# FoX attention on one core: masks of five of eight diagonal blocks moved into copies of the gates, and the low halves of K kept in fixed slots

## The chip, the core and the metric

The kernel runs on one core of a Trainium2 chip. Times are microseconds of device time of one execution; three runs of the kernel before gave a median of 2348.22 (2346.97 to 2348.58). A profile is one further execution, recorded by the hardware: it names each instruction's engine, line, start and duration. The engines are PE (TensorE: matrix products, with its weight loads PEld), DVE (VectorE), ACT (ScalarE), POOL (GpSimd) and SP, which here only issues transfers (DMAs). Each engine works through its own list of instructions in order, and waits at semaphores for the others.

## What is computed

A trunk of two layers over 1024 frames of width 1024, in float32: layer 0 mixes by FoX attention, layer 1 by gated linear attention (GLA), each followed by a SwiGLU layer, all with RMS norm and adaLN modulation from a vector c. The change is in the FoX attention, 16 heads of 64:

```python
log_f = jax.nn.log_sigmoid(f_logit.astype(jnp.float32) + b_f.astype(jnp.float32))
cum = jnp.cumsum(log_f, axis=1).transpose(0, 2, 1)
scale = FOX_HEAD_DIM ** -0.5
for blk in range(S // Q_BLOCK):
    qs, qe = blk * Q_BLOCK, (blk + 1) * Q_BLOCK
    logits = jnp.einsum('bqhd,bkhd->bhqk', q[:, qs:qe], k[:, :qe]).astype(jnp.float32) * scale
    logits = logits + cum[:, :, qs:qe, None] - cum[:, :, None, :qe]
    mask = (qs + jnp.arange(Q_BLOCK))[:, None] >= jnp.arange(qe)[None, :]
    logits = jnp.where(mask[None, None], logits, -jnp.inf)
    p = jax.nn.softmax(logits, axis=-1).astype(v.dtype)
    outs.append(jnp.einsum('bhqk,bkhd->bqhd', p, v[:, :qe]))
```

Query block qb (0 to 7) of 128 rows sees the key blocks 0 to qb; only the last of them, the diagonal block of 128 x 128, needs the mask.

## The kernel before

**Heads and units.** Heads come in pairs p = 0 to 7, with a = 0, 1 for the two heads of a pair, so head h = 2p + a. `attention(p)` goes through the units of a head in the order g = 0, 3, 1, 2 (`ORDER`); a unit holds the query blocks 2g and 2g + 1. So a head goes through blocks 0, 1, then 6, 7, then 2, 3, then 4, 5, and block 5 is the last. The outputs of a unit are held back (`pending`) until the scores of the next unit stand in the program.

**A block's scores.** `scores` cuts the keys of a block into pieces of at most 512 columns (block 4 into 384 and 256; blocks 5 to 7 into 512 and the rest). Each piece is made by two products, Q with the high half of K (L1292, tiles KA or KB for the two heads of a pair) and with the low half (L1293, KLA or KLB). The tiles of K are 128 rows high, of which the other head's 64 rows are zero. A piece that ends with the diagonal block gets a third product on PE, identb times maskb (L1295), which adds 1e30 above the diagonal. DVE then adds the gates, a row of cum spread over 128 partitions, takes the running minimum and writes the piece to lp (L1298); ACT takes exp (L1302), DVE the reciprocal of the sum (L1303), POOL scales the block (L1304). PE transposes the scaled block (L1324, lp to t_b), ACT and DVE split it into a high and a low half (L174, L175, to pt), and PE multiplies with V (L1336, L1338, to o_b). Of o_b's two halves ACT copies one (L1352, to ot) and DVE adds the other and writes oT (L1353).

**What runs beside it.** `weave` lays the program of `attention(p)` and the projections of q, k and v for the next pair (qk_b, vps_b; L316 to L318) into one another by their estimated costs, and a scheduler then sets the final order on each engine. The projections split their weights into halves (L246, on POOL and DVE), `q_evac` and `k_evac` bring q and k out of PSUM (L867 to L883), and each call of `k_evac` writes zeros into the empty half of KLA and KLB first (L877, L878, POOL). Between them stands the modulation of the later parts, which multiplies loaded pieces of in_ada_w (L477, L479 on POOL, L516 on DVE, tiles ada and acc).

**Gates.** `load_cum` (L1119) lets SP load the row of one head, 1024 numbers spread over 128 partitions, 512 KB as written, into one of two buffers. It is called for heads 0 and 1 at the end of the gates, and for the two heads of the next pair after the program of a pair.

**Constants.** maskb holds 1e30 above the diagonal in bf16; tri is the 0/1 triangle that the GLA layer uses much later.

## Time and profile before

| | |
|---|---|
| median of three runs | 2348.22 us (2346.97 to 2348.58) |
| the profiled execution | 2348.03 us, of which 2346.3 is the span from its first to its last instruction |
| mean granted clock of PE | 0.995 |
| attention stage | about 98 to 600 us: the first mask product starts at 98.1, the last at 589.5 |
| mask products, L1295 | 128 loads of identb (96 ns each) and 128 products (230 ns each) |
| scaling of blocks, L1304 | 128 on POOL, 98.2 us |

In rows of the profile, an operation is written with its line, engine, what it writes, an arrow and what it reads, shapes and a count; tile names lose their numbers (lp_s, s_b, t_b: _s for SBUF, _b for PSUM). In timelines the first two columns are the start and the duration in us. What stands in brackets behind a row is the idle time of that engine before it and the instruction that ended it. The durations of products overlap, since PE starts the next one before the last has come out: two starts, not one duration, tell what a product costs.

### The profile page before, as it was taken

What the parts mean: (1) busy time and instruction counts of PE and PEld (TensorE: products, weight loads), DVE (VectorE), ACT (ScalarE), POOL (GpSimd) and SP (SyncE); (2) the same over time, 40 slices, a digit from 0 to 9 for tenths busy, and PEclk for the clock granted to TensorE, in tenths of its full rate; (3) what the DMA queues carried; (4) which work ended last, traced back from release to release, by engine and by line L of the source; (5) the groups of instructions that cost most, each with busy time, mean ns of one, the idle gap of its engine ahead of it and who ended that gap; (6) DMA issues with size and microseconds to landing.
All of it is one profiled execution on the core that took longest, in us unless ns stands there. A gap on an engine that the chain in (4) does not pass through costs nothing.

```text
span 2346.3 us, 35561 instructions
## 1 busy us (share of the span) xinstructions
PE 2326.5 (99%) x12168; PEld 1983.7 (85%) x12168; DVE 1779.5 (76%) x2947; ACT 1123.0 (48%) x2166; POOL 1142.8 (49%) x1005
## 2 busy tenths in 40 slices
PE   8999999999999999999999999999999999999999
PEld 7988888888888888888888899898888888888888
DVE  6577787877687888887788666568787777876787
ACT  6565665665544333345325654345444333345236
POOL 1334455533345656665563522335456666664651
PEclk8999999999999999999999999999999999999999
DMA  8423333432325545448774443554435544458774
GB/s 262 146 79 116 108 113 94 128 127 103 117 95 188 184 162 167 161 172 314 253 272 155 134 129 100 148 174 167 150 106 160 177 150 156 140 189 299 238 267 137
DMA packets 349615, 383.38 MB, mean 163 GB/s; under 512 B 25373, under 2 KB 286649, under 8 KB 349433
## 3 DMA queue, kind: packets, MB, share of 16 engines
q1 hardware_dynamic: 349432, 381.11, 49.3%
q8 instruction: 96, 1.57, 0.3%
q14 instruction: 87, 0.70, 0.1%
HBM read 279.76 MB, written 101.25 MB: 162 GB/s over the span
## 4 chain that ended last, share of the span: by engine, by line
PE 90%; DVE 3%; DMA 3%; issue 1%; SPq 1%; ACT 1%; POOL 1%; DVEq 0%; POOLq 0%; ACTq 0%
PE p_b L316 16%; PE p_b L318 16%; PE p_b L317 16%; PE o_b L1338 2%; PE t_b L1324 2%; PE qk_b L316 2%; PE qk_b L317 2%; PE qk_b L318 2%; PE vps_b L318 1%; PE vps_b L316 1%; PE vps_b L317 1%; PE gr_b L316 1%; PE s_b L1292 1%; PE s_b L1293 1%; PE gr_b L317 1%
## 5 line engine op out<-in xcount | busy, mean ns | idle before, releaser
L174 ACT CAST o_s<-xv_s 128x512 fp32r<-128x512 f32 (+1 forms) x392 | 236.5, 610 | 344.4 <-PE p_b L318 256.9
L175 DVE TENSOR_TENSOR o_s<-xv_s,o_s 128x512 fp32r<-128x512 f32 (+1 forms) x392 | 335.2, 860 | 42.6 <-ACT o_s L174 40.5
L318 PE MATMUL p_b<-B,o_s 128*128 128x512 f32 x608 | 236.0, 389 | 0.0
L317 PE MATMUL p_b<-B,o_s 128*128 128x512 f32 x608 | 235.9, 389 | 0.0
L316 PE MATMUL p_b<-B,o_s 128*128 128x512 f32 x608 | 235.4, 390 | 0.0
L1304 POOL TENSOR_SCALAR lp_s<-lp_s,st 128x128 f32<-128x128 f32 (+7 forms) x128 | 98.2, 771 | 246.1 <-DVE st L1303 231.2
L951 POOL TENSOR_TENSOR ex_s<-xv_s,xv_s 128x512 f32<-128x512 f32 (+1 forms) x64 | 95.6, 1494 | 238.3 <-DMA xv_s<-in_ffn_w_in_dram 118.4
L316 PE MATMUL p_b<-T,o_s 128*128 128x512 f32 x480 | 186.8, 389 | 0.0
L317 PE MATMUL p_b<-T,o_s 128*128 128x512 f32 x480 | 186.7, 389 | 0.0
L318 PE MATMUL p_b<-T,o_s 128*128 128x512 f32 x480 | 181.2, 389 | 0.0
L318 PEld LDWEIGHTS p_b<-B,o_s 128*128 128x128 f32 x608 | 114.1, 188 | 23.9
L316 PEld LDWEIGHTS p_b<-B,o_s 128*128 128x128 f32 x608 | 114.1, 188 | 23.7 <-DVE x L1670 0.2
L317 PEld LDWEIGHTS p_b<-B,o_s 128*128 128x128 f32 x608 | 114.2, 188 | 23.5
L1302 ACT ACTIVATE lp_s<-lp_s,st 128x128 f32<-128x128 f32 (+7 forms) x128 | 99.4, 777 | 57.2 <-DVE st L1298 55.8
L953 POOL TENSOR_TENSOR xv_s<-ex_s,xv_s 128x512 f32<-128x512 f32 (+1 forms) x64 | 94.5, 1477 | 58.9 <-DVE o_s L175 55.9
L1670 DVE TENSOR_TENSOR ex_s<-ex_s,p_b 128x512 f32<-128x512 f32 x140 | 94.2, 681 | 36.7 <-PE p_b L318 36.6
L174 ACT CAST pt_s<-t_b 128x512 fp32r<-128x512 f32 (+1 forms) x160 | 79.7, 547 | 73.7 <-PE t_b L1324 73.1
L963 POOL TENSOR_TENSOR xv_s<-xv_s,xv_s 128x512 f32<-128x512 f32 x48 | 65.5, 1365 | 92.7 <-issue 52.3
L246 POOL TENSOR_TENSOR w_l_s<-w__s,w_h_s 128x256 fp32r<-128x256 f32 x90 | 69.4, 800 | 84.3 <-ACT w_h_s L242 66.3
L175 DVE TENSOR_TENSOR pt_s<-t_b,pt_s 128x512 fp32r<-128x512 f32 (+1 forms) x160 | 96.3, 630 | 15.9 <-ACT pt_s L174 15.4
L318 PEld LDWEIGHTS p_b<-T,o_s 128*128 128x128 f32 x480 | 90.1, 188 | 18.7
L317 PEld LDWEIGHTS p_b<-T,o_s 128*128 128x128 f32 x480 | 90.1, 188 | 18.7
(1527 smaller groups left out, 7413.9 us busy)
## 6 DMA issues: line engine op xcount, KB each, us to landing
xv_s<-in_ffn_w_in_dram SPq DMA_DIRECT2D x176, 256.0 KB, 3.2
hid_B<-x SPq DMA_DIRECT2D x66, 512.0 KB, 2.8
ad_s<-in_ada_w_dram SPq DMA_DIRECT2D x384, 64.0 KB, 2.4
hid_T<-x SPq DMA_DIRECT2D x44, 512.0 KB, 2.9
xv_s<-in_ffn_w_out_dram SPq DMA_DIRECT2D x88, 256.0 KB, 3.8
ada_s<-in_ada_w_dram SPq DMA_DIRECT2D x96, 128.0 KB, 2.7
T2o<-hid_T SPq DMA_DIRECT2D x22, 512.0 KB, 6.6
T1o<-hid_T SPq DMA_DIRECT2D x22, 512.0 KB, 6.3
```

The source lines that it names most:

```text
L174: nc.scalar.copy(hi, src)
L175: nc.vector.tensor_sub(lo, src, hi.bitcast(F32))
L246: (nc.gpsimd if i < 3 else nc.vector).tensor_sub(lo[:, cs], rw[:, cs], hi[:, cs].bitcast(F32))
L316: nc.tensor.matmul(ps, ah, bh, start=start, stop=False, skip_group_check=chain)
L317: nc.tensor.matmul(ps, ah, bl, start=False, stop=False, skip_group_check=chain)
L318: nc.tensor.matmul(ps, al, bh, start=False, stop=stop, skip_group_check=chain)
L951: nc.gpsimd.tensor_add(s1, a21, a22)
L953: nc.gpsimd.tensor_sub(a11, s1, a11)
L963: nc.gpsimd.tensor_sub(r[A12], r[A12], r[A11])
L1302: nc.scalar.activation(lp, lp, AF.Exp, bias=mcur, scale=-1.0, accum_out=st[:, qi, 2:3])
L1304: nc.gpsimd.tensor_scalar(lp, lp, st[:, qi, 3:4], 1.0, op0=ALU.mult, op1=ALU.mult)
L1670: nc.vector.tensor_add(d, d if src is None else dest(G, src), ps)
```

## The change

The masks of query blocks 0, 1, 4, 5 and 7 are no longer added by a product. For those blocks the mask is added on POOL to a copy of the gates, so that DVE's one operation with the gates adds it along. `near` holds the gates of block 0, and of blocks 0 and 1, for query blocks 0 and 1; `far` holds those of key blocks 3, 4 and of 4, 5 for the last pieces of query blocks 4 and 5. Both exist once and are loaded anew for each head by two transfers each, as soon as the head before has used them. For block 7 the mask goes into the last 128 columns of the head's own row of cum. Blocks 2, 3 and 6 keep their product. The rows of cum are now loaded one head at a time, after the last unit of the head that used the buffer. One addition on POOL masks near (128x2x128), one far, and one the end of cum (128x128), for each head.

The low halves of K get fixed slots: KLA serves all pairs, KLB and a new KLC take turns, and their zeros are written once (for pairs 0 and 1). The result of ACT's copy L1352 is written straight into oT, and DVE adds onto it in place. near and far are reused in the GLA layer: tri is made there in near, the states Sf lie in far, and junk in near.

In numbers of instructions: PE loses 80 loads and 80 products; POOL loses 26 memsets and gains 48 additions; SP gains 64 transfers; DVE loses one copy; ACT's number stays.

```diff
@@ -168,7 +168,8 @@
     for q in range(4):
         nc.vector.memset(four[32 * q:32 * q + 32, q:q + 1], 1.0)
     maskb = cst.tile([P, P], BF16, name="maskb")
-    tri = cst.tile([P, P], I32, name="tri")
+    near_t = cst.tile([P, 3 * P], F32, name="near")
+    far_t = cst.tile([P, HALF], F32, name="far")
 
     def split(hi, lo, src):
         nc.scalar.copy(hi, src)
...
@@ -846,20 +841,25 @@
 
     SC = -(64 ** -0.5)
 
-    qk_at = {}
+    qk_at, kl, kl_sl = {}, {}, []
 
     def qk_tiles(p):
 
 
-        at = {nm: qk_free.popleft() for nm in ("QA", "QB", "KA")}
+        at = {nm: qk_free.popleft() for nm in ("QA", "QB")}
         if p:
             before = qk_at.pop(p - 1)
-            at.update(zip(("KB", "KLA", "KLB"), (before[nm] for nm in ("QA", "KA", "KLA"))))
-            qk_free.extend(before[nm] for nm in ("QB", "KB", "KLB"))
+            at.update(KA=before["QA"], KB=before["KA"])
+            qk_free.extend(before[nm] for nm in ("QB", "KB"))
         else:
-            at.update({nm: qk_free.popleft() for nm in ("KB", "KLA", "KLB")})
+            at.update({nm: qk_free.popleft() for nm in ("KA", "KB")})
+        new = {0: ("KLA", "KLB"), 1: ("KLC",)}.get(p, ())
+        for nm in new:
+            kl_sl.append(qk_free.popleft())
+            kl[nm] = big.tile([P, S], FR, tag=kl_sl[-1], name=nm)
         qk_at[p] = at
-        return {nm: big.tile([P, S], FR, tag=sl, name=f"{nm}{p}") for nm, sl in at.items()}
+        t = {nm: big.tile([P, S], FR, tag=sl, name=f"{nm}{p}") for nm, sl in at.items()}
+        return t | {"KLA": kl["KLA"], "KLB": kl["KLC" if p % 2 else "KLB"], "zero": [(kl[nm], nm != "KLA") for nm in new]}
 
     def q_evac(ps, t, hf):
         cs = hsl(hf)
@@ -874,8 +874,8 @@
     def k_evac(ps, t, hf):
         cs = hsl(hf)
         KA, KB, KLA, KLB = t["KA"], t["KB"], t["KLA"], t["KLB"]
-        nc.gpsimd.memset(KLA[64:128, cs].bitcast(F32), 0.0)
-        nc.gpsimd.memset(KLB[0:64, cs].bitcast(F32), 0.0)
+        for z, b in t["zero"]:
+            nc.gpsimd.memset((z[0:64, cs] if b else z[64:128, cs]).bitcast(F32), 0.0)
         nc.scalar.copy(KA[0:64, cs], ps[0:64, :])
         nc.scalar.copy(KB[64:128, cs], ps[64:128, :])
         nc.scalar.copy(KA[64:128, cs], ps[0:64, :])
@@ -1105,6 +1105,8 @@
         nc.sync.dma_start(cum_d, cum)
         load_cum(0)
         load_cum(1)
+        load_near(0)
+        load_far(0)
 
     def v_split(g, tp, ps):
         v = vring([P, 2, 4, 2, 64], FR, f"v{g}{tp}")
@@ -1115,8 +1117,34 @@
     cums = {}
 
     def load_cum(h):
-        cums[h] = cumr([P, S], F32, f"cum{h}")
-        nc.sync.dma_start(cums[h], cum_d[h].partition_broadcast(P))
+        if h < 16:
+            cums[h] = cumr([P, S], F32, f"cum{h}")
+            nc.sync.dma_start(cums[h], cum_d[h].partition_broadcast(P))
+
+    def load_near(h):
+        if h < 16:
+            for o, n in ((0, 1), (P, 2)):
+                nc.sync.dma_start(near_t[:, o:o + n * P], cum_d[h, 0:n * P].partition_broadcast(P))
+
+    def load_far(h):
+        if h < 16:
+            for o, b in ((0, 3), (2 * P, 4)):
+                nc.sync.dma_start(far_t[:, o:o + 2 * P], cum_d[h, b * P:(b + 2) * P].partition_broadcast(P))
+
+    def mask_near(h):
+        if h < 16:
+            mask_pair(near_t, 0)
+
+    def mask_far():
+        mask_pair(far_t, 1)
+
+    def mask_pair(t, b):
+        t = t.rearrange("p (b k) -> p b k", k=P)[:, b:b + 3:2]
+        nc.gpsimd.tensor_add(t, t, maskb.unsqueeze(1).to_broadcast([P, 2, P]))
+
+    def mask_last(h):
+        t = cums[h][:, 7 * P:]
+        nc.gpsimd.tensor_add(t, t, maskb)
 
 
 
@@ -1275,6 +1303,7 @@
         t = qkt[p]
         Qs, K1, KL = (t["QA"], t["KA"], t["KLA"]) if a == 0 else (t["QB"], t["KB"], t["KLB"])
         cm = cums[2 * p + a]
+        own = {0: near_t[:, 0:P], 1: near_t[:, P:], 4: far_t[:, 0:2 * P], 5: far_t[:, 2 * P:]}
         if g < 2:
             both = lpr([P, (4 * g + 3) * P], F32, f"lp{p}{a}{g}")
             lps = [both[:, 0:(2 * g + 1) * P], both[:, (2 * g + 1) * P:]]
@@ -1290,12 +1319,14 @@
                 early = u == (0, 0, 0)
                 diag = k1 == Wd
                 nc.tensor.matmul(ps, Qs[:, qs], K1[:, k0:k1], start=True, stop=False)
-                nc.tensor.matmul(ps, Qs[:, qs], KL[:, k0:k1], start=False, stop=not diag)
-                if diag:
+                by_pe = diag and qb in (2, 3, 6)
+                nc.tensor.matmul(ps, Qs[:, qs], KL[:, k0:k1], start=False, stop=not by_pe)
+                if by_pe:
                     nc.tensor.matmul(ps[:, k1 - k0 - P:], identb, maskb, start=False, stop=True)
                 mnew = st[:, qi, n_:n_ + 1]
+                cmk = own[qb] if diag and qb in own else cm[:, k0:k1]
                 with tc.issue_after(v_last) if early else ExitStack():
-                    nc.vector.tensor_tensor_reduce(lp[:, k0:k1], ps, cm[:, k0:k1], 1.0, mcur,
+                    nc.vector.tensor_tensor_reduce(lp[:, k0:k1], ps, cmk, 1.0, mcur,
                                                    ALU.add, ALU.min, mnew)
                 mcur = mnew
                 yield max(0.22, 0.00085 * (k1 - k0))
@@ -1348,9 +1379,10 @@
             yield 0.01
             pv(b)
             yield 0.44
-        ot = sm.tile([64, 256], F32, tag="t1k", name=f"ot{p}{a}{g}")
-        nc.scalar.copy(ot, ops[64:128, :])
-        nc.vector.tensor_add(oTs[p][a * 64:(a + 1) * 64, g * 256:(g + 1) * 256], ops[0:64, :], ot)
+        rows = slice(a * 64, (a + 1) * 64)
+        ot = oTs[p][rows, g * 256:(g + 1) * 256]
+        nc.scalar.copy(ot, ops[64 - a * 64:128 - a * 64, :])
+        nc.vector.tensor_add(ot, ops[rows, :], ot)
 
     ORDER = (0, 3, 1, 2)
     LAGS = dict(P=18)
@@ -1366,9 +1398,21 @@
 
     def attention(p):
         for a in range(2):
-            for g in ORDER:
+            h = 2 * p + a
+            for i, g in enumerate(ORDER):
                 u = (p, a, g)
+                if h and i == 1:
+                    mask_far()
                 lps = yield from scores(u)
+                if i == 0:
+                    if h:
+                        mask_last(h)
+                    load_near(h + 1)
+                elif i == 1:
+                    mask_near(h + 1)
+                elif i == 3:
+                    load_far(h + 1)
+                    load_cum(h + 2)
                 if p:
                     ada0p(0.8)
                 if pending[0] is not None:
@@ -1392,13 +1436,14 @@
     run(v_half(0, 1, lambda: split_after.update((e, last_of(e)) for e in "ADG")))
     in_order(begin)
     v_last = last_of("D")
+    mask_last(0)
+    mask_near(0)
+    mask_far()
     for p in range(7):
         parts = [qk_proj(p + 1, 0), qk_proj(p + 1, 1)]
         if p < 6:
             parts.insert(1, v_half(p // 2 + 1, p % 2))
         weave(attention(p), 23.0, chain(*parts), 31.0 if p < 6 else 20.8, LAGS)
-        load_cum(2 * p + 2)
-        load_cum(2 * p + 3)
     ada0.flush()
     ada0p.flush()
 
...
@@ -2039,6 +2084,11 @@
     nc.vector.memset(rm.rearrange("p (n c) -> p n c", c=P)[:, :, 0:1], 0.0)
     og_d = tc.dram_tile([8, P, S], F32, name="og_d")
     pj, atr, kvr, opr, trr = ps_rings(3, 1, 1, 2, 1)
+    tri = near_t[:, 0:P]
+    nc.vector.memset(tri, 1.0)
+
+    nc.gpsimd.affine_select(out=tri, in_=tri, pattern=[[1, P]], compare_op=ALU.is_ge,
+                            fill=0.0, base=0, channel_multiplier=-1)
     for v_ in atz.v:
         nc.gpsimd.memset(v_, 0.0)
     S_t = big.tile([P, 2, 2, 256], FR, tag=s_slot, name="S_t")
...
```

**PE, at the start of head 6** (blocks 0 and 1 of the head, tiles s_b_73 and s_b_74, with the projections qk_b between; t_b transposes block 4 of head 5 ahead of it, o_b is a product with V). Before:

```order
L1324 MATMUL t_b_60_3328<-ident,lp_s_38_3186 128x128
L1292 MATMUL s_b_73_3267<-KA_2486,QA_2484 128x128
L1293 MATMUL s_b_73_3267<-KLA_2488,QA_2484 128x128
L1295 LDWEIGHTS identb
L1295 MATMUL s_b_73_3267<-maskb,identb 128x128
L316 MATMUL qk_b_25_3382<-h0h_187,w_h_s_25_2746 128x512
L317 MATMUL qk_b_25_3382<-h0l_188,w_h_s_25_2746 128x512
L318 MATMUL qk_b_25_3382<-h0h_187,w_l_s_26_2747 128x512
L1338 MATMUL o_b_23_3234<-pt_s_56_3240,v_s_5_1366 128x256 x4
L1338 MATMUL o_b_23_3234<-pt_s_57_3247,v_s_6_1472 128x256 x2
L1336 MATMUL o_b_23_3234<-pt_s_57_3247,v_s_6_1472 128x128 x2
L1292 MATMUL s_b_74_3295<-KA_2486,QA_2484 128x256
```

After the change:

```order
L1355 MATMUL t_b_60_3304<-ident,lp_s_38_3168 128x128
L1321 MATMUL s_b_73_3244<-KA_2472,QA_2470 128x128
L1323 MATMUL s_b_73_3244<-KLA,QA_2470 128x128
L317 MATMUL qk_b_25_3358<-h0h_185,w_h_s_25_2731 128x512
L318 MATMUL qk_b_25_3358<-h0l_186,w_h_s_25_2731 128x512
L319 MATMUL qk_b_25_3358<-h0h_185,w_l_s_26_2732 128x512
L1321 MATMUL s_b_74_3269<-KA_2472,QA_2470 128x256
L1323 MATMUL s_b_74_3269<-KLA,QA_2470 128x256
L317 MATMUL qk_b_25_3358<-h0h_187,w_h_s_25_2731 128x512
L318 MATMUL qk_b_25_3358<-h0l_188,w_h_s_25_2731 128x512
L319 MATMUL qk_b_25_3358<-h0h_187,w_l_s_26_2732 128x512
L1321 MATMUL s_b_75_3342<-KA_2472,QA_2470 128x512
```

The loads of identb and the mask products of both blocks are gone, and the eight products with V of o_b_23 have moved behind the next piece of scores, s_b_75.

**POOL, at the end of head 3** (lp_s_25 holds blocks 2 and 3, lp_s_26 block 4, lp_s_27 block 5 of head 3, lp_s_28 blocks 0 and 1 of head 4; acc is the modulation; cum_s_6 is the row of gates of head 5, next in the buffer of head 3). Before:

```order
L1304 TENSOR_SCALAR lp_s_25_2280<-lp_s_25_2280,st_2281 128x384
L1304 TENSOR_SCALAR lp_s_25_2280<-lp_s_25_2280,st_2281 128x512
L477 TENSOR_SCALAR acc_s_1_749<-acc_s_1_749,c_164 128x256
L479 TENSOR_TENSOR acc_s_1_749<-acc_s_1_749 128x256
L1304 TENSOR_SCALAR lp_s_26_2387<-lp_s_26_2387,st_2389 128x640
L1304 TENSOR_SCALAR lp_s_27_2388<-lp_s_27_2388,st_2389 128x768
L477 TENSOR_SCALAR acc_s_1_749<-acc_s_1_749,c_164 128x256
L1304 TENSOR_SCALAR lp_s_28_2477<-lp_s_28_2477,st_2478 128x128
```

After the change:

```order
L1335 TENSOR_SCALAR lp_s_25_2275<-lp_s_25_2275,st_2276 128x384
L1335 TENSOR_SCALAR lp_s_25_2275<-lp_s_25_2275,st_2276 128x512
L478 TENSOR_SCALAR acc_s_1_747<-acc_s_1_747,c_165 128x256
L480 TENSOR_TENSOR acc_s_1_747<-acc_s_1_747 128x256
L1335 TENSOR_SCALAR lp_s_26_2379<-lp_s_26_2379,st_2381 128x640
L1147 TENSOR_TENSOR cum_s_6_2430<-cum_s_6_2430,maskb 128x128
L1335 TENSOR_SCALAR lp_s_27_2380<-lp_s_27_2380,st_2381 128x768
L478 TENSOR_SCALAR acc_s_1_747<-acc_s_1_747,c_165 128x256
L1335 TENSOR_SCALAR lp_s_28_2464<-lp_s_28_2464,st_2465 128x128
```

The addition of the mask to the gates of head 5 stands between the scalings of blocks 4 and 5. At the end of head 7 the order is the same.

**POOL and SP, at the end of head 5** (lp_s_38 block 4, lp_s_39 block 5 of head 5, lp_s_40 blocks 0 and 1 of head 6; cum_s_8 is the gates of head 7). POOL before:

```order
L477 TENSOR_SCALAR acc_s_1_749<-acc_s_1_749,c_164 128x256
L479 TENSOR_TENSOR acc_s_1_749<-acc_s_1_749 128x256
L1304 TENSOR_SCALAR lp_s_38_3186<-lp_s_38_3186,st_3188 128x640
L1304 TENSOR_SCALAR lp_s_39_3187<-lp_s_39_3187,st_3188 128x768
L1304 TENSOR_SCALAR lp_s_40_3265<-lp_s_40_3265,st_3266 128x128
L1304 TENSOR_SCALAR lp_s_40_3265<-lp_s_40_3265,st_3266 128x256
```

POOL after the change:

```order
L480 TENSOR_TENSOR acc_s_1_747<-acc_s_1_747 128x256
L478 TENSOR_SCALAR acc_s_1_747<-acc_s_1_747,c_165 128x256
L1335 TENSOR_SCALAR lp_s_38_3168<-lp_s_38_3168,st_3170 128x640
L480 TENSOR_TENSOR acc_s_1_747<-acc_s_1_747 128x256
L1147 TENSOR_TENSOR cum_s_8_3214<-cum_s_8_3214,maskb 128x128
L1143 TENSOR_TENSOR far<-far,maskb 128x2x128
L1335 TENSOR_SCALAR lp_s_39_3169<-lp_s_39_3169,st_3170 128x768
L1335 TENSOR_SCALAR lp_s_40_3242<-lp_s_40_3242,st_3243 128x128
L1335 TENSOR_SCALAR lp_s_40_3242<-lp_s_40_3242,st_3243 128x256
L1143 TENSOR_TENSOR near<-near,maskb 128x2x128
```

Now the additions to cum of head 7 and to far of head 6 both stand ahead of the scaling of block 5, and that to near ahead of the modulation. SP before:

```order
L227 DMA w__s_33_3525<-in_fox_w_in_dram 128x8x128
L227 DMA wv_0_s_34_3771<-in_fox_w_in_dram 128x4x256
L1119 DMA cum_s_8_3263<-cum_d 128x1024
L453 DMA ada_s_35_3985<-in_ada_w_dram 32x4x256 x4
L1365 DMA oT_d<-oT_s_3_2622 128x1024
L453 DMA acc_s_1_749<-in_ada_w_dram 32x2x256 x4
```

SP after the change:

```order
L228 DMA w__s_33_3500<-in_fox_w_in_dram 128x8x128
L1132 DMA far<-cum_d 128x256
L228 DMA wv_0_s_34_3747<-in_fox_w_in_dram 128x4x256
L1122 DMA cum_s_8_3214<-cum_d 128x1024
L1132 DMA far<-cum_d 128x256
L1127 DMA near<-cum_d 128x128
L1127 DMA near<-cum_d 128x256
L454 DMA acc_s_1_747<-in_ada_w_dram 32x2x256 x4
```

Ahead of and behind the row of cum, SP now issues the two pieces of far, then the two of near, and only then the pieces of the modulation.

13 lines of the change are left out of this document (4 added, 9 removed).

## The prediction

> **What bounds the kernel now.** I read the page's first and fourth parts first, then a table of stretches, then what its waits say, and last the timeline around one mask and around three ends of a head.
>
> ```profile
> span 2346.3 us, 35561 instructions
> PE 2326.5 (99%) x12168; PEld 1983.7 (85%) x12168; DVE 1779.5 (76%) x2947; ACT 1123.0 (48%) x2166; POOL 1142.8 (49%) x1005
> PE 90%; DVE 3%; DMA 3%; issue 1%; SPq 1%; ACT 1%; POOL 1%; DVEq 0%; POOLq 0%; ACTq 0%
> ```
>
> TensorE is busy over 99% of the span and makes 90% of the chain that ended last. The profiled execution took 2348.03 us, 1.7 more than its span, and 0.2 less than the median of 2348.22; the sum below starts from 2348.0. The change touches the attention stage, about 98 to 600 us, so the table of stretches is read there (length, then busy time and count of PE, PE's loads, DVE, ACT and POOL, then the granted clock).
>
> ```profile
> 90.00:150.00 60.00, 59.28 (x403) 53.01 (x402) 36.11 (x96) 34.46 (x73) 25.23 (x36) 1.00 0.30 87
> 270.00:330.00 60.00, 59.85 (x402) 53.51 (x401) 48.81 (x123) 37.39 (x81) 29.38 (x43) 1.00 0.37 114
> 390.00:450.00 60.00, 58.03 (x394) 51.66 (x393) 48.31 (x122) 34.37 (x76) 31.57 (x46) 1.00 0.38 114
> 450.00:510.00 60.00, 58.25 (x351) 49.26 (x350) 47.07 (x124) 41.39 (x86) 21.99 (x33) 1.00 0.38 124
> ```
>
> PE fills 59 to 60 of every 60 us at a granted clock of 1.00 up to 390; DVE, the next engine, needs 49 at most in these rows. Only from 390 to 510 does PE stand idle for something to speak of: 1.97 + 1.75 = 3.7 us. So work taken off PE shortens this stage, as long as the others deliver in time. POOL is half idle, but it stands in a chain that PE waits on: scores (PE), reduce (DVE L1298), exp (ACT), reciprocal (DVE L1303), normalise (POOL L1304), transposes (PE L1324).
>
> ```profile
> L1304 POOL TENSOR_SCALAR lp_s<-lp_s,st 128x128 f32<-128x128 f32 (+7 forms) x128 | 98.2, 771 | 246.1 <-DVE st L1303 231.2 <-PE o_b L1336 9.4 <-PE t_b L1324 3.9
>   POOL lp_s L1304: 6.4, 7
> ```
>
> The first row: POOL's idle time is nearly all waiting for that chain. The second, from the view of line L1324, says that PE's transposes waited for L1304 only 6.4 us in seven places. The chain is close behind PE, seldom ahead of its bound.
>
> **The change, part by part.**
>
> **PE loses 80 masks.** Five of eight diagonal blocks over 16 heads lose the load of identb and the product.
>
> ```profile
> L1295 PE MATMUL s_b<-maskb,identb 128*128 128x128 bf16 x128 | 29.4, 230 | 0.0
> 200.61 0.34 PE L1293 MATMUL s_b<-KLB,QB 128*128 128x384 f32 x1
> 200.79 0.23 PE L1295 MATMUL s_b<-maskb,identb 128*128 128x128 bf16 x1
> 200.82 0.47 PE L317 MATMUL qk_b<-h0l,w_h_s 128*128 128x512 f32 x1
> 201.14 0.39 PE L318 MATMUL qk_b<-h0h,w_l_s 128*128 128x512 f32 x1
> 201.36 0.39 PE L316 MATMUL qk_b<-h0h,w_h_s 128*128 128x512 f32 x1
> ...
> 104.53 0.33 PE L1292 MATMUL s_b<-KA,QA 128*128 128x384 f32 x1
> 104.70 0.34 PE L1293 MATMUL s_b<-KLA,QA 128*128 128x384 f32 x1
> 104.89 0.23 PE L1295 MATMUL s_b<-maskb,identb 128*128 128x128 bf16 x1
> 104.95 0.28 PE L1324 MATMUL t_b<-ident,lp_s 128*128 128x128 f32 x1
> ```
>
> Products overlap, so the 230 ns of one is not its price. I compare starts. A 384-column product is followed after 0.17 (104.53 to 104.70), a 512-column one after 0.22 (201.14 to 201.36). Without the mask, L1293 at 200.61 and L317 would bring the next start to 200.61 + 0.17 + 0.22 = 201.00; it was at 201.14, so the mask costs 0.14, partly its own step and partly a slower product behind it. Bounds: from the mask to the next start there are 0.03 (200.79 to 200.82) and 0.06 (104.89 to 104.95), and its whole duration is 0.23. That is 2.4 to 18.4 us for 80. I take 0.13, next to the worked case: **10.4 us**.
>
> [...]
>
> **POOL loses 26 memsets and gains 48 additions**, 16 of 128x128 and 32 of 128x2x128.
>
> ```profile
> L877 POOL MEMSET KLA<- x16: 519/520/523, 73.4 to 500.3; 64x512 f32 x16
> L479 POOL TENSOR_TENSOR acc_s<-acc_s 128x256 f32<-128x256 f32 x31 | 22.9, 739 | 1.4
> ```
>
> Memsets: 26 x 0.52 = 13.5 us off. Additions: 32 x 0.74 from the 128x256 addition and 16 x about 0.4 (half the size, an estimate) = 30 us on. As busy time both lie in POOL's idle half; it is where they stand in its queue that counts.
>
> **SP gains 64 transfers** (near 16 + 16, far 32); the 16 of cum stay.
>
> ```profile
> acc_s<-in_ada_w_dram SPq DMA_DIRECT2D x64, 64.0 KB, 2.4
> ada_s<-in_ada_w_dram SPq DMA_DIRECT2D x96, 128.0 KB, 2.7
> cum_s<-cum_d SPq DMA_DIRECT2D x16, 512.0 KB, 4.2
> 227.29 0.34 SPq L1119 DMA_DIRECT2D cum_s<-cum_d  x1
> DVE acc_s L516 <- DMA ada_s<-in_ada_w_dram: 14.3, 11, 2.2
> ```
>
> At 0.34 us an issue, 64 fill 22 us of SP's queue over 500. A far piece is 128 KB as written: I take the 2.7 of the row of that size, between 2.4 and 4.2. A far or near waits on SP for the reduce that reads the old piece, and behind it wait the ada and weight loads; before, only the cum transfers did so, at every second end of a head. I take nothing for it: a late ada load holds DVE (last row: 14.3 us in 11 places, 2.2 at most), and PE's queue of products covers that nearly everywhere; where the cover is gone, as ahead of 414.50 (below), one place costs 2.0.
>
> **Ends of heads 3, 5 and 7.** Here an addition that waits for its transfer stands on POOL ahead of the normalise of query block 5. Rows of DVE, POOL and PE for head 3, then 5:
>
> ```profile
> 226.54 0.08 DVE L1298 DVE_READ_ACCUMULATOR2_ANT st<- 128x1 f32 x1
> 230.30 0.91 POOL L1304 TENSOR_SCALAR lp_s<-lp_s,st 128x768 f32<-128x768 f32 x1 [4.76 <-DVE st L1303]
> 231.26 0.44 PE L1324 MATMUL t_b<-ident,lp_s 128*128 128x128 f32 x2
> ...
> 290.19 0.09 DVE L1298 DVE_READ_ACCUMULATOR2_ANT st<- 128x1 f32 x1
> 292.27 1.76 POOL L1304 TENSOR_SCALAR lp_s<-lp_s,st 128x768 f32<-128x768 f32 x3 [3.36 <-DVE st L1303]
> 293.32 0.50 PE L1324 MATMUL t_b<-ident,lp_s 128*128 128x128 f32 x3
> ```
>
> In head 3 the normalise ends at 231.21 and PE follows at 231.26: no slack. In head 5 the first of three ends near 293.18 for PE's 293.32. After the change, in head 3 the cum transfer can go once the first cut of block 5 is reduced (226.62). It lands at 226.66 + 4.2 = 230.9; the addition takes 0.4, the normalise 0.91: 232.2, against 231.26. With the shortest landing of the cum view, 3.4, it is 231.4. So 0.1 to 1.0 late, and I take 0.7, and the same in head 7, where the order of POOL is that of head 3 (an estimate by that likeness). In head 5 the second far piece goes after the last reduce (290.28), at about 290.3, lands at 293.0, and is followed by 0.74 and 0.91: 294.65, against 293.32 less the 0.13 of a mask: **1.5** late. By 2.4 it is 1.2, by 4.2 it is 3.0. Behind the addition are queued the normalises of the next head's first unit; PE waits for them through the same queue. Sum of the three ends: 2.9.
>
> **The start.** POOL's first splits began at 93.61; the new additions of heads 0 and 1 stand ahead.
>
> ```profile
> 93.61 2.50 POOL L246 TENSOR_TENSOR w_l_s<-w__s,w_h_s 128x256 fp32r<-128x256 f32 x3 [18.02 <-issue]
> 101.81 0.96 POOL L1304 TENSOR_SCALAR lp_s<-lp_s,st 128x128 f32<-128x128 f32 x2 [1.34 <-DVE st L1303]
> ```
>
> The splits move by the transfers' landing and four additions, some 3.7 us as I estimate; 1.34 of it are idle time, so the first normalises end at 102.77 + 2.4 = 105.1. PE's transposes are at 104.95 (shown above): 0.2 to 0.6 late, I take 0.4. Bounds: 0 if the transfers land sooner, and 3.
>
> **Where DVE sets the pace.** From 390 to 510 PE already waits. A quarter of the masks (120 of 490 us, 20) stand there, worth 2.6; I count 1.0 of it as lost, between 0 and 2.6. The longest of these waits, 1.97 us ahead of 414.50, may go or stay; I let it stay.
>
> ```profile
> 414.50 0.55 PE L1324 MATMUL t_b<-ident,lp_s 128*128 128x128 f32 x3 [1.97 <-POOL lp_s L1304]
> ```
>
> **At nothing:** the copy written into oT in place (the same instructions on ACT and DVE), and the moved tri, Sf and junk of the later layer, whose order on PE, POOL and SP is the same.
>
> Sum: 2348.0 - 10.4 + 2.9 + 0.4 + 1.0 = 2341.9, about **2342**.
>
> **The rivals.**
>
> *All of the 10.4 arrives*: the additions find their data in time and the chain moves with PE. For it: POOL idles 246 us ahead of L1304. Against it: no slack at head 3. 2348.0 - 10.4 = 2337.6; with half of the 1.97 wait gone too, 2336.6.
>
> *The mask is cheaper*, nearer to the 0.06 from its start to the next: 80 x 0.06 = 4.8, less the same losses of 4.3: 2347.5. For it speaks the second place above, against it the 0.14 of the first. [...] A variant with the same time: the mask is worth 0.13, but other ends of heads lose what 3, 5 and 7 do. For it: twelve more ends of heads have new additions on POOL, and a faster PE takes slack from each. That gives 2343.5 to 2348.
>
> *Slower: the additions hold POOL's queue.* A far or cum addition that waits for a late transfer stops every normalise behind it.
>
> ```profile
> DMA to landing us min/median/max: 3.4/4.2/6.5
> 231.64 0.82 POOL L1304 TENSOR_SCALAR lp_s<-lp_s,st 128x128 f32<-128x128 f32 x2
> 234.65 0.49 PE L1324 MATMUL t_b<-ident,lp_s 128*128 128x128 f32 x3
> ```
>
> The first row is the landing of cum before. At its longest, 6.5, head 5 loses 3.8 more, heads 3 and 7 each 2.3 more. At the four other odd ends the additions stand ahead of the next head's first normalises: there 227.3 + 0.34 + 6.5 + 0.74 + 0.82 = 235.7 (times of head 3), against PE's transposes of head 4 at 234.65, 1.05 each, 4.2 in all. 2341.9 + 8.4 + 4.2 = 2354.5. It decides from landings of about 6 us on; against it, a far piece is a quarter of a cum row.
>
> *That the change doesn't do what it says*: the order of PE shows 80 masks fewer, so this has no chance of its own.
>
> **How the numbers follow.** Forecast, 2339.5 to 2343.5: 0.42. All arrives: 0.15. Cheaper masks or more late ends: 0.35. Slower: 0.08. About 0.2%, 4.7 us, is what a measurement can tell from no change: faster 0.57, same 0.35, slower 0.08. The range goes from 2336.5 (the full price and half of the 1.97) to 2349.5, which leaves out most of the slower case and a little below.
>
> **What would show it.** L1295 falls from 128 to 48 products, and PE's busy time in 90 to 600 by about 10 us: that tests the price. If the time falls by less, the waits of L1324 for L1304 rise from 6.4 us, and the rows at the ends of heads 3, 5 and 7 show POOL idle ahead of an addition, released by a far or cum transfer. If the view of the added transfers shows landings above 6 us, the slower case is on. The forecast is wrong if these waits stay where they were and the time is above 2345, or if new waits stand at ends that I gave nothing.

## The result, and the profile after

The changed kernel took 2360.77 us (median of 5 runs, 2360.3 to 2362.93), against 2348.58 (2346.97 to 2350.56) for the kernel before on the same chip: a ratio of 1.0056 (95% interval 1.0044 to 1.0067). It is slower by 12 to 13 us; the forecast was 2342, with a range of 2336.5 to 2349.5.

The first part of the page of the changed kernel, then rows of its table of stretches of 60 us (length, busy time and count of PE, PE's loads, DVE, ACT, POOL, then the granted clock) with the sum over 90 to 600, and last that sum for the kernel before:

```profile
span 2361.2 us, 35549 instructions
PE 2329.5 (99%) x12088; PEld 1984.9 (84%) x12088; DVE 1770.6 (75%) x2946; ACT 1124.6 (48%) x2166; POOL 1158.1 (49%) x1027
```

```profile
210.00:270.00 60.00, 57.49 (x374) 50.98 (x373) 43.05 (x112) 37.30 (x80) 30.93 (x45) 0.97 0.39 117
270.00:330.00 60.00, 56.73 (x366) 50.84 (x366) 42.83 (x115) 33.31 (x73) 29.25 (x42) 0.94 0.35 107
...
390.00:450.00 60.00, 56.44 (x350) 49.10 (x349) 42.23 (x114) 32.53 (x71) 29.34 (x44) 0.94 0.43 116
...
sum 510.00, PE 492.84 PEld 432.52 DVE 368.37 ACT 302.05 POOL 236.10; mean PE 54.76 PEld 48.06 DVE 40.93 ACT 33.56 POOL 26.23
```

```profile
sum 510.00, PE 504.45 PEld 442.66 DVE 381.31 ACT 306.65 POOL 224.43; mean PE 56.05 PEld 49.18 DVE 42.37 ACT 34.07 POOL 24.94
```

Two things are new. PE stands idle in stretches where it was full, and its granted clock is below 1.00 in three of them. Over 90 to 600 PE is idle for 510 - 492.84 = 17.2 us, before for 510 - 504.45 = 5.6. So 11.6 us more of waiting. The clock: 60 x (0.03 + 0.06 + 0.06) = 9.0 us by this rounded column, and 8.5 by rows of 3 us, as shown below; the kernel before lost none.

Lines have other numbers in the changed kernel: the scaling of a block is L1335, the transposes L1355, the additions L1147 (row of cum) and L1143 (near and far), and the modulation L478 and L480 on POOL and L517 on DVE. The view of the transposes' line tells how late the stage ends, before and after (durations, then first and last start):

```profile
L1324 PE MATMUL t_b<-ident,lp_s x576: 270/272/331, 105.0 to 598.3; 128*128 128x128 f32 x192
```

```profile
L1355 PE MATMUL t_b<-ident,lp_s x576: 270/272/476, 105.2 to 610.0; 128*128 128x128 f32 x192
```

The stage ends 11.7 us later. With +11.6 of waiting and +8.5 of slow clock, what remains is 8.4 us less work on PE for 80 masks (about 0.1 each). This is a remainder and not a measurement of its own. The sign that the prediction named for the price, PE's busy time in 90 to 600 falling by about 10 us, came out as 11.6, but it doesn't test the price: the later stage pushes work out of this window, and the slow clock lengthens products in it (512 columns: 0.63 us at 300.69, 0.39 us in the kernel before). The rest of the 14.9 us between the two spans lies behind the attention, where the profiled executions of all runs here, changed or not, differ by up to 3.5 us; nothing is read into it.

What the engines waited for in the attention stage, in all, how often, and at longest, of the changed kernel:

```profile
POOL cum_s L1147 <- DMA cum_s<-cum_d: 38.0, 9, 19.0
POOL acc_s L478 <- DMA acc_s<-in_ada_w_dram: 24.3, 7, 4.7
DVE acc_s L517 <- DMA ada_s<-in_ada_w_dram: 21.9, 8, 4.9
POOL near L1143 <- DMA near<-cum_d: 9.5, 8, 3.4
POOL far L1143 <- DMA far<-cum_d: 3.9, 4, 2.5
```

```profile
  POOL lp_s L1335: 15.4, 16
```

POOL waited for the rows of cum nine times. The first, 19.0 us, lies ahead of the attention and holds nothing there; most of the rest is at ends of heads. DVE's waits for ada, 14.3 us before with 2.2 at most, have grown to 21.9 with 4.9 at most; POOL's for its own pieces from 10.0 to 24.3. The last row is from the view of the transposes' line: PE and its weight loads, counted together, waited there for the scaling on POOL 15.4 us in 16 places, before 6.4 in seven.

The end of head 5, timelines of SP, POOL, PE and the clock:

```profile
291.24 0.34 SPq L1122 DMA_DIRECT2D cum_s<-cum_d  x1
291.88 0.82 SPq L1132 DMA_DIRECT2D far<-cum_d  x1
292.79 2.06 SPq L1127 DMA_DIRECT2D near<-cum_d  x2
301.18 2.48 SPq L454 DMA_DIRECT2D acc_s<-in_ada_w_dram  x4
```

```profile
296.50 0.43 POOL L1147 TENSOR_TENSOR cum_s<-cum_s,maskb 128x128 f32<-128x128 f32 x1 [4.87 <-DMA cum_s<-cum_d]
296.89 0.67 POOL L1143 TENSOR_TENSOR far<-far,maskb 128x256 f32<-128x256 f32 x1
297.53 1.71 POOL L1335 TENSOR_SCALAR lp_s<-lp_s,st 128x768 f32<-128x768 f32 x3
```

```profile
295.49 0.23 PE L1325 MATMUL s_b<-maskb,identb 128*128 128x128 bf16 x1
298.50 1.97 PE L1355 MATMUL t_b<-ident,lp_s 128*128 128x128 f32 x8 [2.77 <-POOL lp_s L1335]
300.12 0.78 PE L317 MATMUL qk_b<-h0h,w_h_s 128*128 128x512 f32 x1
300.69 0.63 PE L318 MATMUL qk_b<-h0l,w_h_s 128*128 128x512 f32 x1
301.12 0.63 PE L319 MATMUL qk_b<-h0h,w_l_s 128*128 128x512 f32 x1
```

```profile
294.00:297.00 3.00, 1.63 (x11) 1.33 (x11) 1.20 (x7) 0.97 (x3) 0.50 (x2) 1.00 0.62 224
297.00:300.00 3.00, 1.50 (x7) 1.51 (x8) 0.03 (x1) 0.51 (x1) 3.00 (x6) 0.54 0.02 7
300.00:303.00 3.00, 3.00 (x13) 2.71 (x12) 2.88 (x7) 2.68 (x7) 2.02 (x4) 0.50 0.06 21
303.00:306.00 3.00, 3.00 (x22) 2.81 (x21) 1.72 (x4) 2.21 (x4) 1.17 (x2) 0.82 0.22 66
```

The row of cum is issued at 291.24 and is used at 296.50, 5.3 us later. The second piece of far, issued at 291.88, landed later still, at 296.75 (4.9 us, the longest of its view), just ahead of its own addition. Behind the waiting addition stand the addition to far and the scaling of block 5; PE waits 2.77 us. Then the clock is granted at 0.54, 0.50 and 0.82: products of 512 columns start 0.43 us apart (300.69 to 301.12), where in the kernel before, at a clock of 1.00, it was 0.22 (201.14 to 201.36). In these nine us 3 x (0.46 + 0.50 + 0.18) = 3.4 us are lost on top of the wait.

The end of head 3 went another way. There the addition waited 4.89 us for the row of cum, but PE did not wait for the scaling of block 5 behind it. PE's wait was for the scaling of block 4, which ended at 227.72 and stands ahead of the addition:

```profile
227.78 0.82 PE L1355 MATMUL t_b<-ident,lp_s 128*128 128x128 f32 x3 [1.09 <-POOL lp_s L1335]
```

The clock fell behind this wait too, to 0.66 and 0.77 in the next six us, 1.7 us. At the end of head 7 PE waited 0.40 us for the scaling of block 5.

At the end of head 9 PE waited for DVE, and DVE for a piece of ada (SP, DVE, PE, clock):

```profile
411.63 6.45 SPq L454 DMA_DIRECT2D ada_s<-in_ada_w_dram  x8
419.83 2.04 DVE L517 SCALAR_TENSOR_TENSOR acc_s<-ada_s,c,acc_s 128x256 f32<-128x256 f32 x4 [4.61 <-DMA ada_s<-in_ada_w_dram]
422.41 0.50 PE L1321 MATMUL s_b<-KB,QB 128*128 128x512 f32 x1 [1.95 <-DVE st L1329]
```

```profile
423.00:426.00 3.00, 1.92 (x9) 1.21 (x7) 2.81 (x8) 2.96 (x7) 0.88 (x1) 0.59 0.74 217
426.00:429.00 3.00, 2.46 (x7) 1.88 (x8) 2.81 (x7) 1.26 (x3) 0.00 (x0) 0.50 0.46 121
```

In the three us after these rows the clock is at 0.78; in all 3.4 us are lost. SP issued these pieces so late because a load of weights ahead of them waited for a split on POOL that ended at 411.16. POOL was late from a wait for near (1.86 us, at 397.60) and two for its own pieces of the modulation (3.09 and 2.34). Before, the pieces of ada were issued from 401.37.

### The profile page after: what moved, and what is told of

The parts are those of the page before. It is cut to its first block, busy times and chain, and to the rows that moved or that the text cites. A ratio compares the mean times of both kernels' runs of the same rounds, so it can differ in the third digit from the quotient of the medians.

```text
span 2361.2 us, 35549 instructions
## 1 busy us (share of the span) xinstructions
PE 2329.5 (99%) x12088; PEld 1984.9 (84%) x12088; DVE 1770.6 (75%) x2946; ACT 1124.6 (48%) x2166; POOL 1158.1 (49%) x1027
## 4 chain that ended last, share of the span: by engine, by line
PE 68%; DMA 3%; DVE 2%; POOL 1%; SPq 1%; ACT 1%; issue 1%; POOLq 0%; DVEq 0%; ACTq 0%
PE p_b L317 16%; PE p_b L318 16%; PE p_b L319 16%; PE gr_b L317 1%; PE gr_b L319 1%; PE gr_b L318 1%; PE gv_b L317 1%; PE gv_b L319 1%; PE gv_b L318 1%; SPq L454 1%; DMA ex_s<-hid_T 1%; DMA og_s<-og_d 1%; DMA pw_s<-in_gla_w_out_dram 1%; PE f1a_b L317 0%; PE f1a_b L319 0%
## 5 line engine op out<-in xcount | busy, mean ns | idle before, releaser
L1335 POOL TENSOR_SCALAR lp_s<-lp_s,st 128x128 f32<-128x128 f32 (+7 forms) x128 | 99.6, 783 | 189.4 <-DVE st L1334 170.3
L318 PEld LDWEIGHTS p_b<-B,o_s 128*128 128x128 f32 x608 | 114.1, 188 | 23.5
L319 PEld LDWEIGHTS p_b<-T,o_s 128*128 128x128 f32 x480 | 90.1, 188 | 18.7
L318 PEld LDWEIGHTS p_b<-T,o_s 128*128 128x128 f32 x480 | 90.1, 188 | 18.6
L317 PEld LDWEIGHTS p_b<-T,o_s 128*128 128x128 f32 x480 | 90.1, 188 | 18.6
```

What stands on the lines that cost most here:

```text
L317: nc.tensor.matmul(ps, ah, bh, start=start, stop=False, skip_group_check=chain)
L318: nc.tensor.matmul(ps, ah, bl, start=False, stop=False, skip_group_check=chain)
L319: nc.tensor.matmul(ps, al, bh, start=False, stop=stop, skip_group_check=chain)
L1335: nc.gpsimd.tensor_scalar(lp, lp, st[:, qi, 3:4], 1.0, op0=ALU.mult, op1=ALU.mult)
```

## The experiments

The theories after the result. **Theory 1**: additions that wait for their transfer hold POOL's queue ahead of a scaling, and PE. **Theory 2**: the added transfers delay the loads of ada and weights in SP's queue, and through DVE and POOL also PE. **Theory 3**: the masks were worth little to begin with. And how much the slower clock adds. All ratios below are to the kernel before on the same chip in the same job.

**The price of the masks alone.** The kernel before, with five of the eight products of each head dropped:

```diff
-                diag = k1 == Wd
+                diag = k1 == Wd and qb in (2, 3, 6)
```

> The kernel before, with the mask products of blocks 0, 1, 4, 5 and 7 left out and nothing put in their place (those masks are missing). It measures the price of 80 masks on PE alone. If one is worth 0.13 us as I put it: 2348.4 - 10.4 = 2338. If only its own step of 0.06 is saved: 2343.5. If the chain through DVE, ACT and POOL sets the pace and the masks were hidden: 2346 to 2348.

Measured: 2344.57, ratio 0.9987 (0.9978 to 0.9997). Of the 10.4 us, 3 to 4 arrive (1 to 5 by the interval). The attention stage ends at 593.8, 4.5 us earlier than before; PE's idle time from 90 to 600 is 510 - 501.62 = 8.4, 2.9 more than before. The clock stayed at 1.00. So some 7.4 us of work left PE, 0.09 a mask, and two fifths of it came back as waiting. Sums of the same table, of this run:

```profile
sum 510.00, PE 501.62 PEld 440.69 DVE 387.17 ACT 307.04 POOL 227.00; mean PE 55.73 PEld 48.97 DVE 43.02 ACT 34.12 POOL 25.22
```

**All but the masks.** The changed kernel with eight products, without near, far and additions:

```diff
-                by_pe = diag and qb in (2, 3, 6)
+                by_pe = diag
...
-                cmk = own[qb] if diag and qb in own else cm[:, k0:k1]
+                cmk = cm[:, k0:k1]
```

> The changed kernel with all eight masks made by products and no near, far or mask additions: what is left of the change are K's fixed slots, the zeros written once, ot in place, and the row of cum loaded per head. If these parts cost nothing, as predicted: 2347 to 2349, the time of before. If moving cum's load or losing the memsets changes the order for the worse, part of the 12 us shows here: above 2352.

Measured: 2351.51, ratio 1.0016 (1.0007 to 1.0026). The attention stage ends at 598.2, as before. A second measurement of the same kernel:

> All masks by products, no transfers, no additions, a second time, since its first ratio (1.0016) stands against its trace, which ends the attention stage 0.15 us earlier than before. If the slots, the copy in place and the row of cum per head cost nothing: within 0.1% of before. If they do cost, outside the attention: again 1.0010 to 1.0025.

Measured: 2351.66, ratio 1.0006 (0.9997 to 1.0015). Together they leave room for 1 to 4 us, not for 12, and the second interval holds zero. The trace doesn't show it in the attention; where it would come from stays open.

**The order on POOL.** The changed kernel; each addition only behind the POOL instruction traced last:

```diff
-        nc.gpsimd.tensor_add(t, t, maskb)
+        with tc.issue_after(last_of("G")):
+            nc.gpsimd.tensor_add(t, t, maskb)
```

(and in the same way for the pair additions to near and far)

> The changed kernel; each mask addition is only issued behind the POOL instruction that was traced last before it, so that at the ends of heads 3, 5 and 7 none stands ahead of the scaling of block 5. Nothing else is changed. Theory 1, additions that wait for transfers hold POOL's queue and so PE (gains of PE's position lost there in the trace: 2.6 + 7.1 + 1.5 = 11.2 us, the slower clock behind two of them included): 2350, between 2347 and 2353. Theory 2, the added transfers in SP's queue delay the loads of ada and so DVE: nothing gained, 2358 to 2362.

Measured: 2347.97, ratio 1.0002 (0.9992 to 1.0011). In the program only the place of the 48 additions in POOL's queue was set, and 13 us are gone. POOL's waits for transfers ahead of these additions in the stage, and the end of the stage:

```profile
POOL far L1144 <- DMA far<-cum_d: 4.7, 3, 3.7
POOL near L1144 <- DMA near<-cum_d: 1.4, 1, 1.4
```

```profile
L1357 PE MATMUL t_b<-ident,lp_s x576: 270/273/330, 104.7 to 599.3; 128*128 128x128 f32 x192
```

No addition waits for a row of cum in the stage any more, and the stage ends 10.7 us earlier than that of the changed kernel. So theory 1 holds as to the cause of most of the loss. That the time came out as forecast is partly luck, for the forecast put all of it at the ends of heads 3, 5 and 7, where the changed kernel had lost 2.6, 7.1 and 1.5 us against before. This run loses 2.9, 1.8 and 0.5 there: 6.0 us are gained, nearly all at head 5, and none at head 3, where PE waits 1.09 us for the scaling of block 4 as it did with the addition. Another 3.6 come from the end of head 9, which lost 4.6 us and here loses 1.0: POOL is no longer late, and SP issues the pieces of ada from 405.03. The scheduler has also put some loads of ada, of the modulation and of weights in other places of SP's queue, so the place on POOL is not the only thing that differs.

**Transfers without additions.**

```diff
-        nc.gpsimd.tensor_add(t, t, maskb)
+        pass
```

(and the same for the pair additions)

> The changed kernel with all 64 added transfers and without the 48 mask additions (the masks of five blocks are missing). Theory 1 (waiting additions): nothing waits for a transfer on POOL, and the gain of 80 masks comes through: 2338 to 2344. Theory 2 (SP's queue): the waits of DVE for ada stay, and the time stays above 2350.

Measured: 2353.8, ratio 1.0022 (1.0012 to 1.0032). Theory 1's forecast is missed, and theory 2 has a part too: with no addition on POOL that could wait, the kernel is still slower than before. Against the changed kernel (1.0056) leaving the additions out gives 8 of the 13 us. It is also slower than the run before with the additions in a late order, whose interval does not meet this one. The two differ in additions, and with them in what the scheduler made of the other queues; the parts don't add up.

**Neither transfers nor additions.** As the last, and without near and far:

```diff
-                    load_near(h + 1)
...
-                    load_far(h + 1)
```

> The changed kernel without the mask additions and without the 64 transfers of near and far (the masks of five blocks are missing). Against the run with transfers and no additions (2353.8) it gives the price of the transfers. Theory 1, the added transfers in SP's queue delay ada and weights: 2342 to 2346, near the 2344.6 of the kernel before with the five products dropped. Theory 2, the rest of the change (slots, row of cum per head) is what costs: 2350 or more.

Measured: 2344.57, ratio 0.9977 (0.9967 to 0.9987), the first theory's time. The attention stage ends at 593.2. Against the run with transfers the ratios differ by 0.0045, 10.6 us (6 to 15 by the ends of the two intervals).

**Transfers with the old work on PE.** The run with transfers and no additions, with all masks by products (`by_pe = diag`).

> All eight masks by products, no additions, but the 64 transfers of near and far are made and the copies are read. Against the run with all masks by products and no transfers (2351.5) it gives the price of the transfers while PE's work is that of before. Theory 1 (transfers cost by themselves, 8 to 10 us): 2358 to 2362. Theory 2 (they cost only where PE has become faster and the chain has no slack): 2350 to 2354.

Measured: 2361.29, ratio 1.0051 (1.0034 to 1.0068). Against 1.0016 and 1.0006 without the transfers: 8 to 11 us for the 64 transfers and the reading of their copies, and not only where PE is faster. The interval of this run, of four executions, is wide: the price is clear, its size is rough. The rows of waits, without transfers and with them:

```profile
DVE acc_s L517 <- DMA ada_s<-in_ada_w_dram: 14.9, 10, 2.3
POOL acc_s L478 <- DMA acc_s<-in_ada_w_dram: 10.0, 4, 4.1
```

```profile
DVE acc_s L517 <- DMA ada_s<-in_ada_w_dram: 20.9, 11, 5.9
POOL acc_s L478 <- DMA acc_s<-in_ada_w_dram: 14.0, 4, 6.2
```

DVE stands at an operation whose ada piece has not landed, up to 5.9 us, and behind it in its queue stand the reduces of the scores. In the timeline of this run SP issues the pieces of ada at 217.20; DVE waits for them until 223.19 (1.94 us), and the reduce of block 4 comes at 225.63. Without the transfers they were issued at 214.42, before at 215.45.

**Transfers that wait for no reader.** As the last, but DVE reads cum, and the transfers are held to their places in SP's queue:

```diff
-                cmk = own[qb] if diag and qb in own else cm[:, k0:k1]
+                cmk = cm[:, k0:k1]
...
+                with tc.issue_after(next(i for i in reversed(nc.cur_bb.bb.instructions) if i.engine == mybir.EngineType.SP)):
```

> As the run with all masks by products and 64 added transfers (2361.3), but DVE reads the gates from cum, so no transfer of near or far waits for a reader; they stand in SP's queue close to the same places, between the loads of ada and weights. If it is the waits on SP ahead of ada and weights that cost: near the run without transfers (2351.5), 2349 to 2354. If the 64 transfers cost by their issue time or their traffic: 2358 to 2362.

Measured: 2357.98, ratio 1.0030 (1.0018 to 1.0042). This lies at the lower edge of the second range, and below the 2361.3 with the waits. Against the two runs without transfers it is 3 to 6 us, where the waits for readers were part of 8 to 11. But the transfers don't go free of waits here: SP waited ahead of them for the transfer before into the same tile to land:

```profile
SPq L1128 <- DMA near<-cum_d: 15.2, 8, 3.8
SPq L1134 <- DMA far<-cum_d: 8.3, 4, 3.1
```

These are 23.5 us, beside some 66 for DVE, the reader, in the run before. So the waits for readers are a part of the price and not the whole of it, and what the transfers would cost with no wait at all was not measured. DVE waits even longer for ada here, 25.6 us in 12 places. Landings of far and near in this run, and of cum:

```profile
cum_s<-cum_d SPq DMA_DIRECT2D x16, 512.0 KB, 4.5
...
far<-cum_d SPq DMA_DIRECT2D x32, 128.0 KB, 5.0
near<-cum_d SPq DMA_DIRECT2D x16, 128.0 KB, 5.4
near<-cum_d SPq DMA_DIRECT2D x16, 64.0 KB, 4.3
```

Here a piece of a quarter of the size of cum's row lands no sooner than that row; in the changed kernel it did for far (3.2 against 4.8). Whether the ada loads behind them are late by issue time, by traffic, or by where the scheduler now puts them is not settled.

**Copies made on the chip.** near and far are made on POOL from the row of cum that is there, so that no transfer is added and no addition waits for one; every such operation is queued behind the POOL instruction traced last, and far is made after the first unit of its own head:

```diff
-            for o, n in ((0, 1), (P, 2)):
-                nc.sync.dma_start(near_t[:, o:o + n * P], cum_d[h, 0:n * P].partition_broadcast(P))
+            c = cums[h].rearrange("p (b k) -> p b k", k=P)
+            t = near_t.rearrange("p (b k) -> p b k", k=P)
+            with tc.issue_after(last_of("G")):
+                nc.gpsimd.tensor_copy(t[:, 1], c[:, 0])
+                nc.gpsimd.tensor_add(t[:, 0:3:2], c[:, 0:2], maskb.unsqueeze(1).to_broadcast([P, 2, P]))
```

> The changed kernel with near and far made on POOL out of the row of cum that is there already (16 copies of 128 columns, 16 of 256, and the same additions), each behind the POOL instruction traced last, so that neither a transfer is added nor an addition waits for one. If waiting additions and added transfers are the whole of the loss, it comes near the run without both: 2344 to 2347. If POOL's extra work in the chain costs by itself: 2350 or more.

Measured: 2345.63, ratio 0.9983 (0.9974 to 0.9992). A second measurement of the same kernel:

> The version with near and far made on POOL from cum, a second time and with more rounds, since its first ratio (0.9983, 0.9974 to 0.9992) lies near what can be told from no change. If the gain is real: 0.9975 to 0.9990. If it was chance: 1.000 within 0.001.

Measured: 2343.74, ratio 0.9980 (0.9971 to 0.9989). This beats both kernels: 4 to 6 us under the one before. It does the whole of what the change set out to do, with 32 more operations on POOL, so POOL's busy time was never the trouble. Waits of this version (from the first of the two), and its stage:

```profile
DVE acc_s L517 <- DMA ada_s<-in_ada_w_dram: 12.4, 8, 3.1
POOL acc_s L478 <- DMA acc_s<-in_ada_w_dram: 9.7, 3, 4.1
```

```profile
L1360 PE MATMUL t_b<-ident,lp_s x576: 270/272/331, 105.2 to 595.4; 128*128 128x128 f32 x192
```

The waits for loads of ada and of the modulation are back to those of before, and the stage ends 2.9 us earlier than before.

**What a stall costs.** The kernel before, with scalings by 1.0 added behind that of block 5 of head 5, PE's order unchanged (3, then 1):

```diff
+            for _ in range(3 if (p, a, qb) == (2, 1, 5) else 0):
+                nc.gpsimd.tensor_scalar(lp, lp, 1.0, 1.0, op0=ALU.mult, op1=ALU.mult)
```

> The kernel before, with three more scalings by 1.0 on POOL behind that of block 5 of head 5, some 2.7 us ahead of PE's transposes, in an unchanged order of PE. It measures what one stall of PE of about 2.6 us costs. If only the stall counts: 2351. If PE's clock falls behind it, as it did for about 6 us behind the 2.8 us stall of the changed kernel (granted 0.5 there): about 3 us more, 2354.

Measured: 2356.38, ratio 1.0027 (1.0016 to 1.0039), 6.3 us. PE's wait, longer than I had meant since other POOL work came between the scalings, and the clock behind it:

```profile
297.27 0.99 PE L1326 MATMUL t_b<-ident,lp_s 128*128 128x128 f32 x7 [4.08 <-POOL lp_s L1306]
```

```profile
297.00:300.00 3.00, 2.73 (x15) 2.46 (x16) 1.82 (x6) 2.09 (x5) 0.25 (x2) 0.73 0.00 0
300.00:303.00 3.00, 3.00 (x18) 2.81 (x18) 2.06 (x7) 2.81 (x6) 2.08 (x3) 0.70 0.00 0
303.00:306.00 3.00, 3.00 (x25) 2.73 (x24) 2.83 (x7) 0.57 (x3) 1.02 (x1) 1.00 0.31 98
```

The clock takes 3 x (0.27 + 0.30) = 1.7 us; with the 4.1 of the wait this is the 5.9 by which head 6 starts later against head 5. The price of this wait is more than its length. A second spell of slow clock, at about 421 to 425 us, is in this run and not in the kernel before: the clock is at 0.71 and 0.72 from 420 to 426, 3 x (0.29 + 0.28) = 1.7 us. The stage ends 6.2 us later than before in all (604.5 against 598.3).

> The kernel before with one more scaling by 1.0 behind that of block 5 of head 5, in an unchanged order of PE and DVE; three of them gave a stall of PE of 4.1 us and 5.9 us at the end of the head. One gives a stall of about 1.3 us. If a stall costs its own length only: 1.2 us, 2351 beside a before of 2350. If even a short stall brings PE's clock down: 3 us or more.

Measured: 2349.65, ratio 0.9995 (0.9986 to 1.0004). PE waits 0.91 us, the clock stays at 1.00, and head 6 starts 1.1 us later; over the whole kernel that can't be told from nothing.

## Why the prediction was wrong

Two terms of the sum failed. The 64 transfers stood at nothing and cost 8 to 11 us in a run of their own. The ends of heads 3, 5 and 7 stood at 2.9 us and lost 11.2, most of it at head 5, where the landing came late and the slow clock behind the wait was not in the sum. Beside these, the path from POOL over SP and DVE to PE at the end of head 9 was not seen. The terms don't add up to the 12 us, since the added transfers also take part in the losses at the ends of heads.

- **PE bounds the stage**: right. Work taken off PE alone (the first experiment) gives 0.13%, and with the slots, ot in place and the row of cum per head beside it (the run without transfers and additions) 0.23%.
- **80 masks at 0.13, 10.4 us**: a little too large as a price. The three accounts give 0.09 to 0.12: 8.4 us in the changed kernel (above), 7.4 with only the products dropped, and without transfers and additions 5.1 earlier at the end of the stage + 0.8 more idle + 3.4 of slow clock (by rows of 3 us) = 9.3. The larger error is the step behind it: I let nearly all of it reach the end, with 1.0 lost where DVE sets the pace. 3 to 4 are lost, as waits and as slow clock, before any addition or transfer is made.
- **48 additions hidden in POOL's idle half**: right as to busy time, shown by the version with copies on the chip.
- **64 transfers at nothing**: wrong, and shown by itself: 8 to 11 us. I saw that ada loads would stand behind the new transfers and took the cover of PE's queue as enough, at 2.0 a place where it is gone. It was gone in many places: DVE's waits for ada grew by half in the changed kernel (14.3 to 21.9 us).
- **Ends of heads 3, 5 and 7, 2.9 us**: the mechanism was right at head 5, and the size far too small. From PE's transposes of each head against those of before, the three ends lost 2.6, 7.1 and 1.5 us, 11.2 in all. At head 5 I had the far piece issued at 290.3 and landed at 293.0; it was issued at 291.88 and landed at 296.75, after 4.9 us and not 2.7. The row of cum, which I left out of this sum, was used at 296.50, and its addition stood first, so that it was cum's wait that held POOL. And I priced a wait at its own length: 3.4 of the 7.1 are the clock behind it. At head 3 the place was right by luck: PE did not wait for the scaling behind the addition, and 2.9 and 2.8 us are lost there with the additions late and with none at all. Some 1.9 of the 7.1 at head 5 are not the additions' either, since the runs with them late or without them lose 1.8 and 1.9 there. At head 7 PE waited 0.40, where I had 0.7.
- **The start, 0.4**: 0.2 (105.2 against 105.0). **The 1.97 us ahead of 414.50 stays**: it grew. DVE waited 4.61 us for ada there, PE 1.95 and a little later 0.97 and 0.53, and the clock fell to 0.50 again (the end of head 9, above).
- **The slower rival** had the mechanism and the sign. I let it decide only from landings of about 6 us on. It decided at 4.8 (the median of cum, 4.1 to 6.9; far 3.2, near 4.1, at longest 7.4), because the waits also cost clock (8.5 us in the stage) and because the transfers cost by themselves (8 to 11 us in a run of their own). Its 0.08 was too little.
- **Slots, ot in place, row of cum per head at nothing**: 1.0016 and 1.0006, so at nothing or at a few microseconds. With the five masks dropped the same parts went with 0.9977, against 0.9987 without them, which speaks for nothing; the intervals overlap, and it stays open.

What the order showed ahead of the run was enough to see the costliest place: at the end of head 5 an addition with a fresh transfer stood ahead of a scaling with hardly any slack. What was missing is the clock: PE's wait of 2.77 us there took 3.4 us more.

## What to carry to other kernels

Of an instruction that waits for a transfer, look at its place in the queue before its duration: on an engine that stands in the chain of a bound engine, put it behind the work that others wait for, or take its input from what is already on the chip (here the ratio fell from 1.0056 to 1.0002 with the first and to 0.998 with the second). A transfer that is added to a shared queue can be paid by the loads behind it (with 64 of them DVE's waits for ada went from 14.9 to 20.9 us, and the kernel took 8 to 11 us more), so name them and who waits for them. When the bound engine is freed of work, look first at which chain behind it has no slack; that chain takes its part of the gain (2.9 of 7.4 us with the products dropped).

## What the runs showed of the hardware

A wait of PE can be followed by a slow clock: after 2.77 us of idle time the granted clock was 0.50 to 0.82 for nine us, after 4.08 us it was 0.70 to 0.73 for six; after 0.91 us, and after the 1.97 us of the kernel before, it stayed at 1.00. The length of the longest wait alone does not decide it. The clock also fell to 0.50 where that was 1.95 us, with 0.97 and 0.53 behind it (head 9 of the changed kernel), and to 0.66 and 0.77 behind 1.09 us, with 0.28 behind it after three transposes (head 3). In the run without transfers and additions it fell to 0.50 in the row of 411 to 414, behind 1.21 us of idle time in the row of 408 to 411, and no single wait of a product was longer than 0.7 us in that run's stage. Several short waits close together stand ahead of the last three; that they are the cause was not tested. By rows of 3 us, each of these spells took 1.7 or 3.4 us from PE. Three of them cost the changed kernel 8.5 us, beside 11.6 of added waits.
